# Three engines put in program order through the expert chunks, with weight splits traced one unit ahead and gather blocks spread out

## The chip, the core and the metric

The kernel runs on one core of a Trainium2 chip. The metric is the device time of one execution in microseconds (us), and a kernel's time is the median of several executions. A profile of one more execution gives the trace from which the rows below are taken. TensorE (PE) does the matrix products, its weight loads are listed apart as PEld, ScalarE is ACT, VectorE is DVE, GpSimd is POOL, and SyncE (SP) issues the large transfers from HBM.

## The reference, cut to what matters

Two layers are computed for 256 latent tokens (and 256 context tokens) of width 1024. Each layer has a mixer with four branches and then a channel mixer. The channel mixer of the first layer is dense; that of the second routes each token to two of eight experts:

```python
def swiglu(h, w1, w3, w2):
    return (jax.nn.silu(h @ w1) * (h @ w3)) @ w2

def moe_swiglu(h, router, w1, w3, w2):
    logits = (h @ router).astype(jnp.float32)
    top_v, top_i = lax.top_k(logits, TOP_K)          # TOP_K = 2
    probs = jax.nn.softmax(top_v, axis=-1)
    combine = ...                                    # (tokens, 8), zero where an expert wasn't chosen
    out = jnp.zeros_like(h)
    for e in range(N_EXPERTS):                       # 8
        out = out + combine[..., e:e + 1] * swiglu(h, w1[e], w3[e], w2[e])
    return out
```

An expert's w1 and w3 are 1024 x 3584 and its w2 is 3584 x 1024, all float32, so the eight experts hold 352 MB of weights, and each weight is read once. A final RMSNorm follows.

## The kernel before

The first part of the span does the mixers and the dense channel mixer. The change touches the second part only (`moe`), which begins with routing and then walks through the experts' weights.

**Experts and chunks.** The experts are put in slots by their load. Slots 1 to 3 are *heavy* (up to 128 tokens each), slots 0 and 4 to 7 are *light* (up to 64 tokens). Each expert's hidden width of 3584 is cut into seven chunks of 512. A chunk is six *units* of 1 MB: two of w1, two of w3, two of w2. The list `steps` puts the 56 chunks in one order: five light ones first, then heavy and light ones in turn, now and then two light ones in a row. No heavy chunk follows another directly, and two light chunks end the list.

**A light chunk** uses its raw float32 weights as they land (`light_first`: w1 and w3, 64 short matmuls in the trace's count, L1146; `light_turn`: two transposes, L1159, copied out by ScalarE, L1161; `light_second`: w2, 16 matmuls, L1173). Its gate is a Silu on ScalarE (L1150) and a product on VectorE (L1152).

**A heavy chunk** splits each weight unit in two float32r parts. `split` does it in halves of 128x1024: ScalarE copies (rounds) the half into `s1` (L145), then VectorE writes the remainder to `s2` (L146). Each product is then three matmuls (`mm3`, L176, L181, L182): high by high, high by low, low by high. L176 needs ScalarE's part of the split, L181 VectorE's. There are four buffers of `s1` and four of `s2`, so two units can be held split. `moe_first` multiplies w1 (two units), then w3 (two units), with Silu (L1096) and product (L1094). `moe_turn` transposes the result (L1105); ScalarE copies it to `G1` (L1108), VectorE takes the rest to `G2` (L1109). `moe_second` multiplies w2 (two units) into the banks `y`.

**How chunks interlock.** Work is late by a chunk on purpose: when heavy chunk c starts, the turn of heavy chunk c-1 comes first (`turns(True)`), then w1 of c, then in `heavy_aside(1)` the turn of the pending light chunk and w2 of c-1, then w3 of c. The w2 of a light chunk comes at the start of the next light chunk. At a light chunk's end, when a heavy one follows, the two w1 units of the heavy chunk are loaded and split in advance (`self.pre`). When an expert is done, `scatter` or `light_scatter` scales its `y` and adds it to the tokens (L1185 to L1210). The tokens of later experts are gathered (`gather`: eight blocks of four short matmuls, L1058, with XE and XL written by ScalarE and VectorE, then transposes); before, three such steps run after units 0, 2 and 3 of a heavy chunk.

**What sets the order.** Weights land in a ring of ten 1 MB buffers (`raw`, `mraw`); SP issues the next load when the buffer's last reader is done. A light unit's reader is TensorE; a heavy unit's is the split. TensorE's chunk matmuls and turns keep program order (`self.keep`), but everything on ScalarE and VectorE, and TensorE's gather and scatter matmuls, is laid in an order by a scheduler that simulates the kernel while it is built. `high_priority` moves loads and splits ahead in it. On the chip each engine then runs its own list from top to bottom.

Of the kernel before, what the change touches and what calls it, by code (L numbers as in the profile page):

```python
# [49 lines left out]
class Net:  # L50
# [1031 lines left out]
    def moe_first(self, src, XE, c, aside=lambda n: None):  # L1082

        nc = self.nc
        g = self.t2()
        for n, name in enumerate(("m_w1", "m_w3")):
            ps = self.bank(tag="mm")
            for kh in range(2):
                w = self.split_unit(src(name, c, kh))
                for kk in range(4):  # L1090
                    k = 4 * kh + kk
                    self.mm3(ps, (XE[:, 0, k], XE[:, 1, k]), w(512 * kk, 512 * kk + 512), k == 0, k == 7)
                if n == kh == 1:
                    nc.vector.tensor_tensor(g, g, ps, op=ALU.mult)  # L1094
                elif kh == 1:
                    nc.scalar.activation(g, ps, AF.Silu)  # L1096
                aside(2 * n + kh)
        return g

    def moe_turn(self, g):  # L1100

# [7 lines left out]
        nc.vector.tensor_tensor(G2, pt, G1.bitcast(F32), op=ALU.subtract)  # L1109
        return G1, G2  # L1110

    def moe_second(self, src, c, G, y, last=False, aside=lambda: None):
        G1, G2 = G
        for hb in range(2):
            self.cut = 2 if last and hb + self.ncut > 1 else 1
            w = self.split_unit(src("m_w2", c, hb))
            self.cut = 1
            for b in range(2):
                j = 2 * hb + b
                for hf in range(2):  # L1120
                    o = 1024 * b + 512 * hf
                    self.mm3(y[hf], (G1[:, j], G2[:, j]), w(o, o + 512), c == 0 and j == 0, c == EFF_CH - 1 and j == 3)
            if hb == 0:
                aside()

# [93 lines left out]
    def moe(self):  # L1219
        nc, E = self.nc, self.E  # L1220
        XE, PT, ready = {}, {}, set()

        def tables(i):
            tabs = (self.pos, self.sel, self.comb) if i == 0 else self.placed
            return [a[:, :2, i:i + 1] for a in tabs]

        def light(i, P):

            Q = E.tile([128, 2, 128], F32R, tag="Q", name=self.nm("Q"), bufs=1)
            nc.vector.memset(P[:, :, 192:].bitcast(F32), 0.0)  # L1230
            nc.vector.memset(Q[:, :, :64].bitcast(F32), 0.0)
            pos, sel, _ = tables(i)
            self.one_hot(P[:, :, 128:192], pos, sel)
            self.one_hot(Q[:, :, 64:], pos, sel)
            XE[i] = E.tile([128, 8, LCAP], F32, tag="XL", name=self.nm("XL"), bufs=2)
            PT[i] = E.tile([128, 2, 2, 128], F32R, tag="PTL", name=self.nm("PTL"), bufs=2)
            return Q

        def heavy(i, P):
            pos, sel, _ = tables(i)  # L1240
            self.one_hot(P[:, :, :128], pos, sel)
            XE[i], PT[i] = self.xe_tile(), self.pt_tile()

        def turn(i, P, Q=None):
            if Q is None:
                self.turned(PT[i], [P[:, t, :128] for t in range(2)])
            else:
                self.turned(PT[i].rearrange("p t h c -> p (t h) c"), [x for t in range(2) for x in (P[:, t, 128:], Q[:, t])])

        def gather(i, j):  # L1250

            P = E.tile([128, 2, 256], F32R, tag="P", name=self.nm("P"), bufs=1)
            if i:
                heavy(i, P)
            Q = light(j, P)
            yield from self.gather(P[:, :, 0 if i else 128:192], XE.get(i), XE[j])
            if i:
                turn(i, P)
            turn(j, P, Q)
            ready.update((i, j))  # L1260

        def begin():
            yield from gather(None, 0)
            self.weights()
            self.by_load()
            yield
            yield from gather(1, NH + 1)

        def run(gen, n=1000):
            for _ in range(n):  # L1270
                if next(gen, self) is self:
                    break

        big = lambda i: 0 < i <= NH
        side = begin()
        run(side, 9)
        hs, ls = ([(i, c) for i in p for c in range(EFF_CH)] for p in (range(1, NH + 1), [0, *range(NH + 1, NE)]))

        n = self.lead
        rest = [((k + 0.5) / len(q) * f, x) for q, f in ((hs, 0.95), (ls[n:], 1)) for k, x in enumerate(q)]  # L1280
        steps = ls[:n] + [x for _, x in sorted(rest, key=lambda a: a[0])]
        more = {(NH + k, 2): (k + 1 if k < NH else None, NH + k + 1) for k in range(1, NE - NH - 1)}

        def source(i):
            if i == 0:
                return lambda name, c, j: self.d[name][0, c, j]
            return lambda name, c, j, e=self.ids[i]: self.d[name][bass.ds(e, 1), c, j].rearrange("a p c -> (a p) c")
        y, g, G, late = {}, {}, {}, []
        todo = {True: [], False: []}

        def turns(kind):
            for x in todo[kind]:
                if x in g:
                    G[x] = (self.moe_turn if kind else self.light_turn)(g.pop(x))

        def puts():
            while late:
                run(late.pop(0))

        def second(kind, **kw):  # L1300

            while todo[kind] and todo[kind][0] in G:
                i, c = x = todo[kind].pop(0)
                if c == 0:
                    y[i] = self.ys() if kind else self.bank(tag="yl")
                (self.moe_second if kind else self.light_second)(source(i), c, G.pop(x), y[i], **kw)
                if c == EFF_CH - 1:
                    late.append((self.scatter if kind else self.light_scatter)(PT[i], y[i], tables(i)[2]))
                    run(late[-1], 1)

        def heavy_aside(n):
            if n == 1:
                turns(False)
                puts()
                second(True)
            else:
                run(side, 3)

        for m, (i, c) in enumerate(steps):
            kind = big(i)  # L1320
            if i == 0 and c == 4:
                self.gdma = False
                gf = self.O.tile([128, 2, 1024], F32, tag="gf", name="gf")
                self.g2, self.fg = self.gate(2, 0, gf[:, 0]), gf[:, 1]
                nc.scalar.dma_start(self.fg, self.d["fng"])
            if c == 0 and i not in ready:
                puts()
                run(side)
            after = steps[m + 1] if m + 1 < len(steps) else (0, 0)

            def light_aside(n):
                if n == 1:
                    turns(False)
                if n == 3 and big(after[0]):

                    if after[0] not in ready:
                        puts()
                        run(side)
                    src = source(after[0])
                    self.pre = [self.split_unit(src("m_w1", after[1], kh)) for kh in range(2)]  # L1340

            if kind:
                turns(True)
                g[i, c] = self.moe_first(source(i), XE[i], c, heavy_aside)
            else:
                second(False)
                g[i, c] = self.light_first(source(i), XE[i], c, light_aside)
                if not big(after[0]):
                    second(False)
            todo[kind].append((i, c))  # L1350
            if not kind and todo[True] and not any(big(x) for x, _ in steps[m:]):
                turns(True)
                second(True, aside=lambda: turns(False))
                puts()
            if (i, c) in more:
                puts()
                run(side)
                side = gather(*more[i, c])
        turns(False)
        second(False, last=True)  # L1360
        puts()

    def moe_rest(self):

# [351 lines left out]
```

## Time and profile before

| quantity | value |
|---|---|
| median of three runs | 1717.22 us (1715.92 to 1721.92) |
| the profiled execution's own time | 1717.08 us |
| its span in the trace | 1715.3 us |
| PE busy | 1623.0 us (95%) |
| VectorE busy | 960.1 us (56%) |
| ScalarE busy | 684.7 us (40%) |
| read from HBM | 478.86 MB |
| expert weight loads of 1 MB, issue to landing | 10.6 us (median) |

The span runs from the first to the last instruction; 1.8 us of the execution's own time lies around it. A matmul is counted as busy for longer than it keeps the next one waiting, so "PE busy" is high where PE merely runs. More telling are the stretches in which it waits, the granted clock (1.00 is 2.4 GHz, 0.50 is 1.2 GHz, and a stretch between them mixes the two), and the bytes that land per second. The expert part begins near 830 us and ends near 1702 us.

### The profile page before, as it was taken

What the parts mean: (1) busy time and instruction counts of PE and PEld (TensorE: products, weight loads), DVE (VectorE), ACT (ScalarE), POOL (GpSimd) and SP (SyncE); (2) the same over time, 40 slices, a digit from 0 to 9 for tenths busy, and PEclk for the clock granted to TensorE, in tenths of its full rate; (3) what the DMA queues carried; (4) which work ended last, traced back from release to release, by engine and by line L of the source; (5) the groups of instructions that cost most, each with busy time, mean ns of one, the idle gap of its engine ahead of it and who ended that gap; (6) DMA issues with size and microseconds to landing.
All of it is one profiled execution on the core that took longest, in us unless ns stands there. A gap on an engine that the chain in (4) does not pass through costs nothing. (4 is left out here: it accounts for less than half of the span.)

```text
span 1715.3 us, 23719 instructions
## 1 busy us (share of the span) xinstructions
PE 1623.0 (95%) x9333; PEld 1206.8 (70%) x9333; DVE 960.1 (56%) x1455; ACT 684.7 (40%) x1086; POOL 35.4 (2%) x46
## 2 busy tenths in 40 slices
PE   7999999999999999999899999998999899999986
PEld 4778799887787878899566566665766576665653
DVE  3769555567665697696233455455533464534343
ACT  4654344322222327655243344442533444433341
POOL 1000000000000030000000000000000000000000
PEclk8999999999999999999889999999999999999998
DMA  8543531534444433227899999999899999999992
GB/s 351 205 158 145 202 135 51 203 137 175 172 172 166 181 145 103 99 95 273 355 387 385 418 420 375 420 418 398 343 390 419 419 419 375 418 408 390 381 420 105
DMA packets 69030, 481.55 MB, mean 281 GB/s; under 512 B 8064, under 2 KB 8192, under 8 KB 12336
## 3 DMA queue, kind: packets, MB, share of 16 engines
q1 hardware_dynamic: 68480, 479.43, 70.6%
q8 instruction: 75, 1.23, 0.3%
q10 hardware_dynamic: 432, 0.54, 0.1%
q14 instruction: 43, 0.35, 0.1%
HBM read 478.86 MB, written 1.08 MB: 280 GB/s over the span
## 5 line engine op out<-in xcount | busy, mean ns | idle before, releaser
L146 DVE TENSOR_TENSOR s<-raw,s 128x1024 fp32r<-128x1024 f32 (+1 forms) x350 | 419.1, 1222 | 111.9 <-ACT s L145 110.0
L145 ACT CAST s<-raw 128x1024 fp32r<-128x1024 f32 (+1 forms) x350 | 357.9, 1050 | 275.3 <-PE mm L182 109.0
L176 PE MATMUL mm<-X,s 128*128 128x512 f32 (+1 forms) x672 | 247.1, 368 | 0.0
L181 PE MATMUL mm<-X,s 128*128 128x512 f32 (+1 forms) x672 | 247.0, 368 | 0.0
L182 PE MATMUL mm<-X,s 128*128 128x512 f32 (+1 forms) x672 | 245.8, 367 | 0.0
L1146 PE MATMUL mm<-raw,XL 128*64 128x256 f32 x1952 | 218.4, 380 | 0.0
L1146 PEld LDWEIGHTS mm<-raw,XL 128*64 128x64 f32 x1952 | 139.0, 137 | 81.2 <-issue 15.9
L176 PE MATMUL mm<-s,XE 128*128 128x512 f32 x336 | 141.2, 420 | 24.3 <-ACT s L145 24.3
L181 PE MATMUL mm<-s,XE 128*128 128x512 f32 x336 | 141.8, 422 | 9.5 <-DVE s L146 9.5
L176 PEld LDWEIGHTS mm<-X,s 128*128 128x128 f32 x672 | 126.4, 188 | 27.9 <-issue 6.7
L181 PEld LDWEIGHTS mm<-X,s 128*128 128x128 f32 x672 | 126.7, 189 | 26.0 <-issue 5.9
L182 PEld LDWEIGHTS mm<-X,s 128*128 128x128 f32 x672 | 126.5, 188 | 24.0 <-issue 3.4
L1150 ACT ACTIVATE t<-mm 128x256 f32<-128x256 f32 x35 | 13.4, 383 | 316.6 <-PE mm L1146 316.6
L182 PE MATMUL mm<-s,XE 128*128 128x512 f32 x336 | 139.0, 414 | 0.0
L1173 PE MATMUL yl<-raw,GL 128*64 128x512 f32 x488 | 111.2, 598 | 6.4 <-DVE t L1208 6.0
L1109 DVE TENSOR_TENSOR G<-sm,G 128x512 fp32r<-128x512 f32 x21 | 14.5, 691 | 168.7 <-ACT G L1108 168.7
L176 PEld LDWEIGHTS mm<-s,XE 128*128 128x128 f32 x336 | 67.1, 200 | 43.5 <-ACT s L145 27.8
L1152 DVE TENSOR_TENSOR t<-t,mm 128x256 f32<-128x256 f32 x35 | 14.6, 418 | 145.2 <-PE mm L1146 145.2
L181 PEld LDWEIGHTS mm<-s,XE 128*128 128x128 f32 x336 | 67.3, 200 | 30.5 <-DVE s L146 15.3
L176 PE MATMUL mm<-s,X 128*128 128x256 f32 (+1 forms) x304 | 86.5, 287 | 1.9 <-ACT mix L666 1.9
L181 PE MATMUL mm<-s,X 128*128 128x256 f32 (+1 forms) x304 | 86.0, 284 | 0.3 <-DVE s L146 0.3
L182 PE MATMUL mm<-s,X 128*128 128x256 f32 (+1 forms) x304 | 85.1, 285 | 0.0
(384 smaller groups left out, 2363.5 us busy)
## 6 DMA issues: line engine op xcount, KB each, us to landing
raw<-in_m_w_dram SPq DMA_DIRECT2D x294, 1024.0 KB, 10.6
mraw<-in_mod_w_dram SPq DMA_DIRECT2D x47, 1024.0 KB, 4.8
raw<-in_f_w_dram SPq DMA_DIRECT2D x33, 1024.0 KB, 4.9
mraw<-in_m_w_dram SPq DMA_DIRECT2D x32, 1024.0 KB, 11.7
raw<-in_w_in_dram SPq DMA_DIRECT2D x20, 1024.0 KB, 4.8
raw<-in_w_out_dram SPq DMA_DIRECT2D x8, 1024.0 KB, 4.9
first<-in_m_w_dram SPq DMA_DIRECT2D x8, 512.0 KB, 8.9
once<-in_m_w_dram SPq DMA_DIRECT2D x3, 1024.0 KB, 16.1
```

Source lines behind the costliest of these rows:

```text
L145: self.last = (nc.scalar.copy(s1[:, :h], r), nc.vector.tensor_tensor(s2[:, :h], r, s1[:, :h].bitcast(F32), op=ALU.subtract))
L146: nc.vector.tensor_tensor(s2[:, :h], r, s1[:, :h].bitcast(F32), op=ALU.subtract))
L176: m = mm(out, a[0], b[0], start=first, stop=False)
L181: self.keep(mm(out, a[0], b[1], start=False, stop=False))
L182: self.keep(mm(out, a[1], b[0], start=False, stop=last))
L1109: nc.vector.tensor_tensor(G2, pt, G1.bitcast(F32), op=ALU.subtract)
L1146: self.keep(nc.tensor.matmul(ps[64 * b:64 * b + 64], XL[:, k], w(o, o + 256), start=(k == 0), stop=(k == 7), tile_position=(0, 64 * b)))
L1150: nc.scalar.activation(g, ps, AF.Silu)
L1152: self.keep(nc.vector.tensor_tensor(g, g, ps, op=ALU.mult))
L1173: self.keep(self.nc.tensor.matmul(y[64 * hf:64 * hf + 64], G[:, b, 64 * hb:64 * hb + 64], w(o, o + 512), start=(c == 0 and hb == b == 0), ...
```

## The change

On TensorE, ScalarE and VectorE every instruction traced between the start of the chunk loop and its end gets a dependency on the one traced before it on the same engine, so that the scheduler can only lay them down in the order in which the Python code calls them. (SP and POOL are left to the scheduler.) Since the order of the code now is the order on the engine, the code is rearranged. A list `plan` holds the units that the next heavy chunk needs: w1, w1, w2 and w2 of the chunk before, w3, w3. `look_ahead` takes one and traces its load and its split. Two are traced at the end of the light chunk ahead of the heavy one, and one more after each unit's matmuls. The same is done for the w2 of the last heavy chunk. Gather steps run one after each unit of a heavy chunk, and one in the middle of w2. When an expert's last w2 is done, `second` returns instead of going on to the next expert, and scatters are put after w1 or after w3 of a heavy chunk, or at the very end.

```diff
@@ moe_first
-                w = self.split_unit(src(name, c, kh))
+                w = self.split_ahead(src(name, c, kh))
...
                 elif kh == 1:
                     nc.scalar.activation(g, ps, AF.Silu)
+                self.look_ahead()
                 aside(2 * n + kh)
         return g
+
+    def split_ahead(self, src):
+        return self.pre.pop(0) if self.pre else self.split_unit(src)
+
+    def look_ahead(self):
+
+        if self.plan:
+            src, cut = self.plan.pop(0)
+            pre, self.pre, self.cut = self.pre, [], cut
+            pre.append(self.split_unit(src))
+            self.pre, self.cut = pre, 1
@@ moe_second
-            w = self.split_unit(src("m_w2", c, hb))
+            w = self.split_ahead(src("m_w2", c, hb))
...
+            self.look_ahead()
             if hb == 0:
                 aside()
@@ moe
                     late.append((self.scatter if kind else self.light_scatter)(PT[i], y[i], tables(i)[2]))
                     run(late[-1], 1)
+                    return
 
         def heavy_aside(n):
             if n == 1:
                 turns(False)
                 puts()
-                second(True)
-            else:
-                run(side, 3)
-
+                second(True, aside=lambda: run(side, 1))
+            elif n == 3:
+                puts()
+            run(side, 1)
+
+        self.plan = []
+        traced = nc.cur_bb.bb.instructions
+        begun = len(traced)
...
                     src = source(after[0])
-                    self.pre = [self.split_unit(src("m_w1", after[1], kh)) for kh in range(2)]
+                    self.plan = [(src(x, after[1], kh), 1) for x in ("m_w1", "m_w3") for kh in range(2)]
+                    if todo[True]:
+                        i, c = todo[True][0]
+                        self.plan[2:2] = [(source(i)("m_w2", c, hb), 1) for hb in range(2)]
+                elif n == 3 and todo[True] and not any(big(x) for x, _ in steps[m:]):
+                    i, c = todo[True][0]
+                    self.plan = [(source(i)("m_w2", c, hb), 1) for hb in range(2)]
+                if n == 3:
+                    for _ in range(2):
+                        self.look_ahead()
...
                 second(True, aside=lambda: turns(False))
-                puts()
...
+        puts()
         turns(False)
         second(False, last=True)
         puts()
+
+        last = {}
+        for x in list(traced[begun:]):
+            if x.engine in (mybir.EngineType.PE, mybir.EngineType.Activation, mybir.EngineType.DVE):
+                if x.engine in last:
+                    self.tc.add_manual_dep(x, last[x.engine].name, mybir.DependencyInfo(
+                        mybir.DependencyClass.NoSync, mybir.DependencyReason.DATA), reason="issue_after")
+                last[x.engine] = x
```

The first place is ScalarE's list at the start of a heavy chunk (the fifth of the second heavy expert). `raw_10540` and `raw_10550` are its two w1 units, `G` the copy of the turned chunk before it, and `t_1916<-mm_10571` its Silu. Before:

```order
L1150 ACTIVATE t_1896_10496<-mm_10497 128x256
L1108 CAST G_1914_10566<-sm_10561 128x512
L145 CAST s_1904_10542<-raw_10540 128x1024
L145 CAST s_1906_10546<-raw_10540 128x1024
L145 CAST s_1909_10552<-raw_10550 128x1024
L145 CAST s_1911_10556<-raw_10550 128x1024
L145 CAST s_1921_10604<-raw_10602 128x1024
L145 CAST s_1923_10608<-raw_10602 128x1024
L145 CAST s_1926_10626<-raw_10624 128x1024
L145 CAST s_1928_10630<-raw_10624 128x1024
L1096 ACTIVATE t_1916_10570<-mm_10571 128x512
```

The same place now, where `raw_10584` and `raw_10607` are the w2 units that were `raw_10602` and `raw_10624`:

```order
L1161 ACTIVATE t_1896_10496<-mm_10497 128x256
L145 CAST s_1904_10542<-raw_10540 128x1024
L145 CAST s_1906_10546<-raw_10540 128x1024
L145 CAST s_1909_10552<-raw_10550 128x1024
L145 CAST s_1911_10556<-raw_10550 128x1024
L1120 CAST G_1914_10566<-sm_10561 128x512
L145 CAST s_1919_10586<-raw_10584 128x1024
L145 CAST s_1921_10590<-raw_10584 128x1024
L1096 ACTIVATE t_1916_10570<-mm_10571 128x512
L145 CAST s_1924_10609<-raw_10607 128x1024
L145 CAST s_1926_10613<-raw_10607 128x1024
```

The copy G (L1108, now L1120) stood ahead of the four w1 copies and now stands behind them; the Silu (L1096) stood behind both w2 units and now stands between them.

The second place is ScalarE's list ahead of the last heavy chunk's w2 (`raw_13015` and `mraw_13042` before). Before:

```order
L1150 ACTIVATE t_2446_12961<-mm_12962 128x256
L1108 CAST G_2454_13011<-sm_13006 128x512
L145 CAST s_2457_13017<-raw_13015 128x1024
L145 CAST s_2459_13021<-raw_13015 128x1024
L145 CAST s_2464_13044<-mraw_13042 128x1024
L145 CAST s_2466_13048<-mraw_13042 128x1024
```

And now, where these units are `raw_13005` and `mraw_13015`:

```order
L1161 ACTIVATE t_2446_12961<-mm_12962 128x256
L145 CAST s_2454_13007<-raw_13005 128x1024
L145 CAST s_2456_13011<-raw_13005 128x1024
L145 CAST s_2459_13017<-mraw_13015 128x1024
L145 CAST s_2461_13021<-mraw_13015 128x1024
L1120 CAST G_2464_13031<-sm_13026 128x512
```

Here too G goes from the front of the four copies to their end.

## Rows read from the trace of the kernel before

**Rows 1.** The page, part 2: GB/s in 40 slices of 42.9 us.
```profile
GB/s 351 205 158 145 202 135 51 203 137 175 172 172 166 181 145 103 99 95 273 355 387 385 418 420 375 420 418 398 343 390 419 419 419 375 418 408 390 381 420 105
```

**Rows 2.** The chain that ended last: start us, us, engine, tile, line.
```profile
1653.08 0.23 PE mm L181
...
1661.27 6.91 PE mm L1146 x64
...
1695.02 3.68 PE yl L1173 x16
1698.72 0.68 DVE t L1208
```

**Rows 3.** Stretches: us, busy per engine (instructions), clock, DMA share, GB/s.
```profile
840.00:1681.00 841.00, 787.66 (x4495) 526.76 (x4490) 387.29 (x445) 326.56 (x436) 0.00 (x0) 0.97 0.98 399
915.00:1681.00 766.00, 715.19 (x4039) 483.33 (x4036) 363.97 (x404) 302.76 (x394) 0.00 (x0) 0.97 0.98 402
895.00:900.00 5.00, 5.00 (x24) 4.00 (x23) 4.18 (x4) 3.80 (x6) 0.00 (x0) 1.00 0.46 146
1200.00:1205.00 5.00, 5.00 (x23) 4.03 (x22) 4.46 (x4) 3.63 (x4) 0.00 (x0) 1.00 0.25 64
1680.00:1685.00 5.00, 4.42 (x18) 1.94 (x19) 3.88 (x6) 0.44 (x1) 0.00 (x0) 1.00 0.15 59
```

**Rows 4.** Waits of SP's queue, 915 to 1681: us in total, times, longest.
```profile
SPq L119 <- DVE s L146: 249.3, 89, 8.6
SPq L119 <- PE yl L1173: 142.9, 56, 7.2
```

**Rows 5.** Waits of PE and ACT, 790 to 1715: us in total, times, longest.
```profile
PE mm L176 <- ACT s L145: 24.3, 15, 1.6
PE mm L181 <- DVE s L146: 9.5, 16, 0.8
PE yl L1173 <- DVE t L1208: 6.0, 4, 1.5
PE y L176 <- ACT s L145: 1.6, 1, 1.6
ACT s L145 <- DMA raw<-in_m_w_dram: 3.9, 3, 2.7
```

**Rows 6.** Timeline, a heavy chunk's start with a wait: start us, us, [idle before].
```profile
1292.83 0.66 PE L1105 MATMUL sm<-ident,t 128*128 128x128 f32 x4
1293.52 0.59 ACT L1108 CAST G<-sm 128x512 fp32r<-128x512 f32 x1 [3.65 <-PE sm L1105]
1294.00 3.89 ACT L145 CAST s<-raw 128x1024 fp32r<-128x1024 f32 x4
1295.11 0.49 PE L176 MATMUL mm<-s,XE 128*128 128x512 f32 x1 [1.62 <-ACT s L145]
1296.36 0.50 PE L181 MATMUL mm<-s,XE 128*128 128x512 f32 x1 [0.77 <-DVE s L146]
```

**Rows 7.** Timeline, a heavy chunk's start without a wait.
```profile
1257.76 2.00 ACT L145 CAST s<-raw 128x1024 fp32r<-128x1024 f32 x2
1261.41 0.48 PE L176 MATMUL mm<-s,XE 128*128 128x512 f32 x1
1261.69 0.59 ACT L1108 CAST G<-sm 128x512 fp32r<-128x512 f32 x1 [1.93 <-PE sm L1105]
1267.41 0.60 ACT L1096 ACTIVATE t<-mm 128x512 f32<-128x512 f32 x1 [1.35 <-PE mm L182]
1268.16 4.90 ACT L145 CAST s<-raw 128x1024 fp32r<-128x1024 f32 x5
```

**Rows 8.** Stretches at two heavy starts, PE alone: busy, clock, DMA share, GB/s.
```profile
1294.10:1302.10 8.00, 6.23 (x19) 0.79 1.01 420
1334.10:1342.10 8.00, 6.24 (x27) 1.00 1.00 416
```

**Rows 9.** The page, part 5: VectorE's half of a split, mean ns.
```profile
L146 DVE TENSOR_TENSOR s<-raw,s 128x1024 fp32r<-128x1024 f32 (+1 forms) x350 | 419.1, 1222 | 111.9 <-ACT s L145 110.0
```

More of the change, by code (lines that the diff above doesn't have):

```diff
@@ L1110, in moe_turn, with moe_second @@
         return G1, G2
-    def moe_second(self, src, c, G, y, last=False, aside=lambda: None):
+    def moe_second(self, src, c, G, y, aside=lambda: None):
         G1, G2 = G
         for hb in range(2):
-            self.cut = 2 if last and hb + self.ncut > 1 else 1
-            w = self.split_unit(src("m_w2", c, hb))
-            self.cut = 1
+            w = self.split_ahead(src("m_w2", c, hb))
             for b in range(2):
```

## Prediction, made before the changed kernel was run

> **What bounds the kernel now.** I read the page's bandwidth slices first. The second half of the span moves weights at up to 420 GB/s, with dips to 343 and 364 and a last slice of 105 [rows 1]. So the expert part runs close to the rate of its own loads, yet not at it. The stretches say how far off: from 915 us, when the first heavy chunks are under way, to 1681 us, when the last weights land, 402 GB/s, against 420 in an undisturbed piece [rows 3, 8]. The loss is in a few holes (64 GB/s at 1200 to 1205, 146 at 895 to 900), and TensorE shows 5.00 us of 5 busy in both [rows 3]: loads pause while TensorE works.
>
> What a load waits for is next. SP's queue waits 249.3 us for VectorE's splits and 142.9 us for the light chunks' w2 matmuls [rows 4], the last readers of ring buffers. In the other direction hardly anybody waits for weights: ScalarE's copies waited for landing data three times in all, 3.9 us [rows 5]. So the ring is full of landed units, and TensorE's progress sets the pace.
>
> TensorE's waits are then what matters. Two have one shape: L176 waits for ScalarE's part of a split 15 times, 24.3 us, at most 1.6 each, and L181 for VectorE's part 16 times, 9.5 us [rows 5]. The timeline shows the place, the start of a heavy chunk [rows 6]. ScalarE sits idle 3.65 us for the transposes of the chunk before, because the copy G (L1108) heads its list; the splits of the w1 units, whose data is there, stand behind it. TensorE does the transposes, then waits 1.62 us for the first half's copy and 0.77 us for its remainder. There is a counter-example in the same trace: at another start ScalarE's list had two w1 copies ahead of G (1257.76 against 1261.69), and L176 starts at 1261.41 with no wait [rows 7]. The order alone makes the difference.
>
> Such a wait has an aftermath. In the 8 us around the start of rows 6 the granted clock is 0.79 and 19 matmuls are recorded; around a start where it stayed at 1.00, 27 [rows 8]. Cutting the same stretch around all 15 starts gives 0.79 nine times and 1.00 six times. A mean of 0.79 over 8 us is 3.4 us at 1.2 GHz, so 1.7 us of work lost.
>
> **The change part by part.** The sum is made against the profiled execution, 1717.08 us with a span of 1715.3; the median of 1717.22 is the same within 0.2 us.
>
> *TensorE's side.* (a) G moves behind the four w1 copies on ScalarE, as in rows 7 but for both units. The 15 waits go: 24.3 + 9.5 = 33.8 us. What is late next is G itself: four copies take 3.89 us [rows 6] and can run while the light chunk's last 64 matmuls (6.91 us [rows 2]) still go on, so G comes straight after the transposes, and its reader, w2, starts 24 matmuls (5.6 us at 0.23 [rows 2]) later. (b) At nine starts 1.7 us of half-clock work goes: 15 us; bounds 0 (the clock falls anyway) and 766 x 0.03 / 0.5 / 2 = 23 us (all of the 0.97 of rows 3 at half clock while working). I take 15, from the count. (c) The last heavy chunk's w2 has the same wait once, 1.6 us [rows 5], and about 0.8 behind it as at the others [rows 6]: 2.4. (d) A new light expert's w2 waited four times, 6.0 us, for the scatter to empty its bank [rows 5]. Since `second` now returns when an expert is done, a heavy chunk lies between: 6.0. Together 33.8 + 15 + 2.4 + 6.0 = 57 us; the w2 matmuls that end at 1698.7 [rows 2] could end at 1642 if weights always were there.
>
> *Gathers.* The same 32 matmuls per gather are spread over two heavy chunks instead of one; nothing is added. The new cost could be a wait for bank or copy at each of five blocks a chunk; the chunk's other matmuls stand between blocks, so I put zero, at most 1.2 us for each of three gathers.
>
> *The loads' side.* SP's order of loads stays nearly what it was, and a load still waits for its buffer. At 420 GB/s the bytes from 915 to 1681 need 766 x 402 / 420 = 733 us, so the last weights can land at 1648, not before, if the hole at 895 to 900 (still with TensorE's start-up behind it) stays. That is later than 1642, so the loads are the bound from some point on. TensorE needs 766 - 57 = 709 us for what the loads need 733: it gains 3% on them, and to use up a backlog of some six landed units (15 us at 2.5 us each, 1.05 MB at 420 GB/s) takes 15 / 0.03 = 500 us. For the first 500 us the ring is nearly full, and a gather or a scatter can still make a hole. Of the 33 us of holes I leave 6: last landing 1654; bounds 0 and 15.
>
> The Trainium skill (DMA: Bandwidth & Descriptors, Specifications) gives an HBM limit of about 358 GB/s per core and a fabric ceiling of 435. By the first the same bytes would need 860 us, and nothing could be gained; by the second 708. The trace's 420 contradicts the first, so the floor stays at 733.
>
> *After the last landing.* Now 17.7 us pass from 1681 to 1698.7, since TensorE is behind by a light chunk's matmuls. With TensorE waiting for weights, what follows the last landing is at most the last w2's 3.68 us [rows 2]; the chunk's first part has the two units before it (5 us) to finish. I take 4 (bounds 2, and 8 at half clock). From there to the end of the span it is 1715.3 - 1698.7 = 16.6 us as now; the scatter's order within it changes by less than 1 us.
>
> Sum: 1654 + 4 + 16.6 = 1674.6 span, + 1.8 around it = 1676.4; I say **1677 us**, 40 us faster.
>
> **Rivals.**
>
> *The clock eats part of it.* Once TensorE outruns the loads it must wait for them, and in rows 8 such pauses bring 1.2 GHz. If all 21 heavy starts lose 1.7 us instead of nine, that is 21 us more on TensorE: 1642 + 21 = 1663, later than the loads' 1648. With 4 for the catch-up, 3 for an end at half clock: 1670 + 16.6 + 1.8 = 1688. For it: nine of 15 starts do so now. Against: a wait for a bound load costs nothing by itself, and work that lands meanwhile is done afterwards at full clock. The Trainium skill (TensorE: Matmul & The Clock Gate, HAM oscillation — how this bites in real kernels) describes such a kernel, throttled again at every tile by its wait for DMA; by it this rival is the rule, by the six starts at 1.00 it is not.
>
> *The full floor.* No hole after 915, and the hole at 895 halved (3 us): 1645 + 2 + 16.6 + 1.8 = 1665. Against: three gathers and eight scatters still come in lumps.
>
> *The Silu takes G's place (slower).* In the new list L1096 stands between the two w2 units. It waits for the last w1 matmul, and the second w2 unit's copy waits behind it. Chain: 0.59 for the Silu [rows 7], 3.89 / 4 = 0.97 for a copy [rows 6], 1.22 for its remainder [rows 9], 2.8 us; cover: the first w2 unit's 12 matmuls x 0.23 = 2.8 us and two transposes of the light chunk. The margin is thin. If it fails by today's 2.4 us with the clock's 1.7 behind it in all 21 chunks, 86 us come and 57 go: 1717 + 29 = 1746. It decides from 57 / 21 = 2.7 us per chunk. Against: in rows 7 the list before had the Silu (1267.41) ahead of copies of that w2 unit too, and L176's wait for w2 splits came once in the whole part, at the very end [rows 5].
>
> *It does nothing.* If the w1 units hadn't landed when ScalarE now turns to them, their wait would only change its name: 1717. Against: copies wait for data 3.9 us in all [rows 5].
>
> **How the numbers follow.** Forecast 0.60, own range 1666 to 1690; clock 0.18; full floor 0.10; Silu 0.07, of it 0.05 slower and 0.02 about even; nothing 0.05. Faster is 0.60 + 0.18 + 0.10 = 0.88, same 0.02 + 0.05 = 0.07, slower 0.05; by over 0.3% (5 us) each, about what a measurement can tell here. The range 1660 to 1703 takes in the floor, the clock's rival and half of (a) failing (17 us and the clock behind it).
>
> **What would show it.** Right: the waits of L176 and L181 at heavy starts fall from 33.8 us to a few or turn into waits for DMA; ScalarE's and SP's lists show waits for landing weights well above 3.9 us in the second half; bandwidth from 915 on is at least 412 GB/s; last weights land near 1654; under 6 us lie between that and the last w2 matmul. Wrong: L176 or L181 on `y` waits 21 times behind L1096 (Silu); clock below 0.95 over the part with loads under 410 GB/s (clock); holes as deep as before with the ring full, which would mean that TensorE's waits were not what held the loads.

## The result and the profile after

The changed kernel takes 1691.39 us (median of four runs, 1690.79 to 1692.21), the kernel before, run on the same chip, 1719.1. The ratio is 0.984, 95% interval 0.9819 to 0.9861: faster by 28 us, where 40 were forecast. The profiled execution after has a span of 1689.1 us.

Bandwidth by slices, from the page of the kernel after (part 2, 40 slices of 42.2 us):

```profile
GB/s 363 195 164 150 180 162 51 184 140 189 160 174 138 207 154 101 125 76 205 335 417 315 419 418 413 405 418 419 418 395 398 419 420 412 418 419 419 419 420 168
```

The dips of before (343, 375 and others below 400 [rows 1]) have shrunk to 395 and 398, save one of 315 near 900 us; most slices stand at 417 to 420. The same in stretches, after, with columns as in [rows 3]:

```profile
840.00:915.00 75.00, 70.44 (x426) 41.34 (x424) 18.44 (x37) 19.31 (x38) 0.00 (x0) 0.91 0.89 351
915.00:1660.00 745.00, 709.63 (x4092) 482.50 (x4090) 366.23 (x416) 302.32 (x398) 0.00 (x0) 0.98 1.01 415
1660.00:1665.00 5.00, 5.00 (x50) 3.34 (x48) 0.00 (x0) 0.38 (x1) 0.00 (x0) 1.00 0.29 117
```

From 915 us on 415 GB/s land, before 402 [rows 3]. In the last of these stretches 117 GB/s x 5 us = 0.59 MB come, 1.4 us at 420: the last weights land near 1661.4. From there 11 us pass to the end of the last w2 matmul, 1672.55, and 16.55 more to the end of the span.

TensorE's waits in the expert part, after (us in total, times, longest), which answer to [rows 5]:

```profile
PE mm L1208 <- DVE res L1211: 12.2, 4, 3.1
PE sm L1058 <- DVE P L1047: 10.4, 4, 3.4
PE sm L1073 <- ACT XL L1066: 5.1, 3, 2.3
PE y L176 <- ACT G L1120: 5.0, 1, 5.0
...
PE mm L176 <- ACT s L145: 2.1, 2, 1.6
PE mm L181 <- DVE s L146: 2.0, 3, 0.8
```

The two waits at heavy starts fell from 24.3 and 9.5 us to 2.1 and 2.0. The first four rows, 32.7 us in all, were not there at this size. The other end of the ring, ScalarE and SP after (the second for 915 to 1660):

```profile
ACT s L145 <- DMA raw<-in_m_w_dram: 12.5, 8, 4.7
```
```profile
SPq L119 <- DVE s L146: 171.6, 64, 9.5
...
SPq L119 <- DMA raw<-in_m_w_dram: 92.4, 61, 2.6
```

ScalarE now waits for weights that haven't landed (12.5 us, before 3.9 [rows 5]), and SP waits for transfers in the queue for 92.4 us, where it waited for none in the same stretch before. Its waits for splits fell from 249.3 [rows 4] to 171.6 us. So for a part of the time it is now the transfers that hold up the next load, and no longer their readers.

The start of [rows 6], the same chunk after (timeline: start us, us, instruction, [idle before]):

```profile
1285.92 3.88 ACT L145 CAST s<-raw 128x1024 fp32r<-128x1024 f32 x4
...
1288.97 0.66 PE L1117 MATMUL sm<-ident,t 128*128 128x128 f32 x4
1289.39 0.48 PE L176 MATMUL mm<-s,XE 128*128 128x512 f32 x1
1289.69 0.58 ACT L1120 CAST G<-sm 128x512 fp32r<-128x512 f32 x1
```

The copies start 3 us ahead of the transposes; L176 follows these with no wait, and G comes behind the copies, 0.06 us after the transposes end (1289.63).

### The profile page after: what moved, and what is told of

Read it like the earlier page. It is cut to its first block, busy times and chain, and to the rows that moved or that the text cites. A ratio compares the mean times of both kernels' runs of the same rounds, so it can differ in the third digit from the quotient of the medians.

```text
span 1689.1 us, 23700 instructions
## 1 busy us (share of the span) xinstructions
PE 1608.9 (95%) x9333; PEld 1202.3 (71%) x9333; DVE 955.9 (57%) x1455; ACT 679.7 (40%) x1086; POOL 35.4 (2%) x46
## 5 line engine op out<-in xcount | busy, mean ns | idle before, releaser
L146 DVE TENSOR_TENSOR s<-raw,s 128x1024 fp32r<-128x1024 f32 (+1 forms) x350 | 414.9, 1221 | 272.2 <-ACT s L145 271.6
L145 ACT CAST s<-raw 128x1024 fp32r<-128x1024 f32 (+1 forms) x350 | 355.4, 1050 | 277.6 <-PE mm L181 98.0
L176 PE MATMUL mm<-X,s 128*128 128x512 f32 (+1 forms) x672 | 247.2, 368 | 0.0
L181 PE MATMUL mm<-X,s 128*128 128x512 f32 (+1 forms) x672 | 247.0, 368 | 0.0
L176 PEld LDWEIGHTS mm<-X,s 128*128 128x128 f32 x672 | 126.4, 188 | 27.9 <-issue 6.7
L181 PEld LDWEIGHTS mm<-X,s 128*128 128x128 f32 x672 | 126.7, 189 | 26.0 <-issue 5.9
L176 PE MATMUL mm<-s,XE 128*128 128x512 f32 x336 | 139.2, 414 | 2.2 <-ACT s L145 2.1
L181 PE MATMUL mm<-s,XE 128*128 128x512 f32 x336 | 136.4, 406 | 2.0 <-DVE s L146 2.0
L182 PE MATMUL mm<-s,XE 128*128 128x512 f32 x336 | 135.9, 404 | 0.0
L176 PE MATMUL mm<-s,X 128*128 128x256 f32 (+1 forms) x304 | 86.5, 287 | 2.0 <-ACT mix L666 2.0
L181 PE MATMUL mm<-s,X 128*128 128x256 f32 (+1 forms) x304 | 86.0, 285 | 0.8 <-DVE s L146 0.8
L1184 PEld LDWEIGHTS yl<-raw,GL 128*64 128x64 f32 x488 | 33.0, 137 | 63.6 <-issue 62.0
L176 PEld LDWEIGHTS mm<-s,XE 128*128 128x128 f32 x336 | 65.6, 195 | 17.3 <-ACT s L145 3.1
L181 PEld LDWEIGHTS mm<-s,XE 128*128 128x128 f32 x336 | 65.5, 195 | 17.4 <-DVE s L146 3.1
## 6 DMA issues: line engine op xcount, KB each, us to landing
once<-in_m_w_dram SPq DMA_DIRECT2D x3, 1024.0 KB, 16.1
```

The lines of the kernel that those rows point to most:

```text
L145: self.last = (nc.scalar.copy(s1[:, :h], r), nc.vector.tensor_tensor(s2[:, :h], r, s1[:, :h].bitcast(F32), op=ALU.subtract))
L146: nc.vector.tensor_tensor(s2[:, :h], r, s1[:, :h].bitcast(F32), op=ALU.subtract))
L176: m = mm(out, a[0], b[0], start=first, stop=False)
L181: self.keep(mm(out, a[0], b[1], start=False, stop=False))
L182: self.keep(mm(out, a[1], b[0], start=False, stop=last))
L1184: self.keep(self.nc.tensor.matmul(y[64 * hf:64 * hf + 64], G[:, b, 64 * hb:64 * hb + 64], w(o, o + 512), start=(c == 0 and hb == b == 0), ...
```

## The experiments

Each ratio is to the kernel before on the same chip, with its 95% interval. Medians of runs on different chips differ by up to 3 us for the same kernel (before: 1716 to 1719), so what tells two versions apart is the ratios; a difference of medians is called one.

**The place of G.** In e1 the kernel before is left as it is, but for a hold: `behind` makes the scheduler lay G behind the last weight copy traced before it.

```diff
@@ moe_turn (kernel before)
-        nc.scalar.copy(G1, pt)
+        with self.behind(self.last[:1]):
+            nc.scalar.copy(G1, pt)
```

> The kernel before with one thing altered: ScalarE's copy G of a turned heavy chunk is held behind the last weight copy traced ahead of it, so that it stands behind the four w1 copies. No pins, no new trace order, gathers as before. Theory (the place of G is the cause): the waits of L176 and L181 at heavy starts fall from 33.8 us to under 8, bandwidth from 915 on rises from 402 to at least 413 GB/s, and the time falls by 20 to 32 us (1687 to 1699). Rival (the gain comes from program order as such, or from gathers and scatters being placed otherwise): less than 8 us.

Measured: 1681.02 us, ratio 0.9794 (0.976 to 0.9827), span 1678.4. One hold gives 35 us by the medians, at least as much as the whole change, and more than the 20 to 32 expected. Its waits and its main stretch:

```profile
PE yl L1174 <- DVE t L1209: 6.0, 4, 1.5
PE mm L181 <- DVE s L146: 5.3, 8, 1.4
PE mm L1198 <- ACT Y L1210: 4.9, 2, 2.7
...
PE mm L176 <- ACT s L145: 4.5, 7, 1.1
```
```profile
915.00:1650.00 735.00, 704.63 (x4060) 472.44 (x4056) 363.60 (x408) 302.66 (x393) 0.00 (x0) 0.99 1.01 417
```

L176 and L181 lose 24 us of their 33.8 (9.8 are left, under 8 were expected), and the granted clock goes from 0.97 to 0.99. The other waits stand as they did: the scatter's for Y is 4.9 us in both traces, so there is no sign that the rest of the schedule moved. The wait of the light w2 (6.0 us, part (d) of the forecast) is still there and does no visible harm. Loads land at 417 GB/s.

In e2 the change stays and only G goes back to the front: the turn is called before the two units of the next chunk are looked ahead, so that G and its remainder on VectorE stand ahead of their splits.

```diff
@@ light_aside (kernel after)
                     src = source(after[0])
+                    turns(True)
                     self.plan = [...]
```

> The changed kernel with one thing undone: the turn of the heavy chunk before is traced ahead of the two w1 splits, so G again heads ScalarE's list at a heavy start; everything else of the change stays. Theory (place of G): 20 waits of 1.62 and 0.77 us come back, 40 to 48 us on TensorE, on top of the changed kernel's own new waits (12.2 us on L1208, 10.4 on L1058, 5 on L1073); time 1715 to 1740, no faster than before. Rival (G's place doesn't matter): 1688 to 1696.

Measured: 1765.59 us, ratio 1.0281 (1.0259 to 1.0304). With program order everywhere, the wait of [rows 6] stands at all 21 starts. One of them, and the sums:

```profile
1327.33 0.58 ACT L1120 CAST G<-sm 128x512 fp32r<-128x512 f32 x1 [3.65 <-PE sm L1117]
1327.81 3.89 ACT L145 CAST s<-raw 128x1024 fp32r<-128x1024 f32 x4
...
1328.91 0.50 PE L176 MATMUL mm<-s,XE 128*128 128x512 f32 x1 [1.62 <-ACT s L145]
```
```profile
PE mm L176 <- ACT s L145: 34.0, 21, 1.6
PE mm L181 <- DVE s L146: 15.7, 21, 0.8
```
```profile
915.00:1650.00 735.00, 662.22 (x3665) 447.84 (x3661) 335.33 (x383) 276.26 (x363) 0.00 (x0) 0.95 0.93 378
```

Against the kernel after 74 us come by the medians (70 between the two profiled executions) in 21 places, 3.3 to 3.5 us each. The traces account for 68 of them: 49.7 us of waits where the kernel after has 4.1, and by the granted clock (0.98 to 0.95 over 735 us, rounded rows) 22 us of lost work. The forecast had 48.8 / 15 = 3.3 us per start for the two. The expectation had reckoned with the waits alone, and the time came out 25 us above its range. So G's place is the cause, in both directions, and its price was about right.

**The pins.** In e3 the loop at the end that adds the dependencies is gone; the code's new order stays.

```diff
-        last = {}
-        for x in list(traced[begun:]):
...
-                last[x.engine] = x
```

> The changed kernel without the dependencies that keep program order: new trace order, look-ahead, gathers and returns stay, the scheduler orders the engines. In its list G stands ahead of most w1 copies again. Theory (place of G): the waits of L176 behind L145 come back to 20 us or more, time 1705 to 1722. Rival (the new trace order brings the gain, the pins nothing): 1688 to 1696.

Measured: 1705.2 us, ratio 0.995 (0.9928 to 0.9973). The scheduler puts G ahead of the copies again; ScalarE sits idle for the transposes before all 21 copies G, 76.1 us in all, and in the kernel after before none:

```profile
PE mm L176 <- ACT s L145: 26.7, 18, 1.6
PE mm L181 <- DVE s L146: 12.4, 18, 0.8
```

Order in the code alone brings about a third of the gain; what the pins add is that ScalarE keeps to it. The waits at the gathers and scatters (L1058 for P, L1208 for L1211) are 0.7 and 0.4 us in this trace: they belong to the pins.

**What the floor is.** In e4 the third product of each heavy triple is left out, 504 matmuls x 0.233 us = 117 us of TensorE's work.

```diff
@@ mm3 (kernel after)
         self.keep(m)
+        if self.kept:
+            self.keep(mm(out, a[0], b[1], start=False, stop=last))
+            return
```

> The changed kernel with the third product (low by high) of each heavy triple left out, which takes 21 x 24 x 0.2325 = 117 us of work from TensorE; loads, splits and order stay. Theory (the loads are the bound in the changed kernel): bandwidth from 915 on 418 to 421 GB/s, last landing 1645 to 1656, the time falls by only 8 to 25 us against the changed kernel (1666 to 1683), TensorE waits for landing weights instead. Rival (TensorE is still the bound): the time falls by over 60 us.

Measured: 1679.98 us, ratio 0.9776 (0.9754 to 0.9798): 117 us less work for TensorE gives 11 us. The stretch:

```profile
915.00:1650.00 735.00, 646.21 (x3602) 386.30 (x3600) 365.87 (x416) 302.22 (x398) 0.00 (x0) 0.96 1.01 418
```

418 GB/s at 646 us of TensorE's busy time: the loads are the bound after the change, and 418 to 420 is what they give here.

**The end.** In e5 G of the last heavy chunk goes back ahead of its w2 copies, everything else as after.

```diff
                 elif n == 3 and todo[True] and not any(big(x) for x, _ in steps[m:]):
+                    turns(True)
                     i, c = todo[True][0]
```

> The changed kernel with the last heavy chunk's turn traced ahead of its two w2 splits, so that there alone G comes first again. Theory (G behind splits whose data has not landed costs 5.0 + 0.7 us and a spell at half clock near the end): that wait shrinks to at most 2.4 us, last landing stays near 1661, the time falls by 2 to 7 us against the changed kernel (1684 to 1689). Rival (the end hangs on the last landing, the wait is absorbed): within 1.5 us of it.

Measured: 1687.09 us, ratio 0.9828 (0.9809 to 0.9847). By the intervals that is not told apart from the kernel after (4.3 us by the medians, 2 by the ratios); the trace shows it, the kernel after first:

```profile
1641.00 1.99 ACT L145 CAST s<-raw 128x1024 fp32r<-128x1024 f32 x2 [4.69 <-DMA raw<-in_m_w_dram]
...
1643.49 1.99 ACT L145 CAST s<-mraw 128x1024 fp32r<-128x1024 f32 x2 [0.50 <-DMA mraw<-in_m_w_dram]
...
1645.39 0.58 ACT L1120 CAST G<-sm 128x512 fp32r<-128x512 f32 x1
1646.02 0.79 PE L176 MATMUL y<-s,G 128*128 128x512 f32 x1 [5.01 <-ACT G L1120]
```

And e5:

```profile
1642.23 0.58 ACT L1120 CAST G<-sm 128x512 fp32r<-128x512 f32 x1 [4.70 <-PE sm L1117]
1642.72 1.99 ACT L145 CAST s<-raw 128x1024 fp32r<-128x1024 f32 x2
...
1643.82 0.49 PE L176 MATMUL y<-s,G 128*128 128x512 f32 x1 [1.62 <-ACT s L145]
```

After, G waits behind four copies of weights that are only landing, though its own input was ready at 1641.0; with G first the wait is 1.62 in place of 5.01. The last w2 starts at 1665.54 us in e5, in place of 1668.90.

**The lumps.** In e6 the light scatter is traced one unit earlier, ahead of the look-ahead's splits, a gather's one-hot tiles are traced when it is set up, and its transposes get a step of their own.

```diff
+                if n < kh:
+                    soon()          # puts
                 self.look_ahead()
@@ heavy_aside
                 turns(False)
-                puts()
@@ gather
+            if j > NH + 1:
+                yield
             yield from self.gather(...)
+            if j > NH + 1:
+                yield
@@ steps
                 side = gather(*more[i, c])
+                run(side, 1)
```

> The changed kernel with three new waits taken away: a light expert's scatter is traced ahead of the split that VectorE had in front of its additions (L1208 behind L1211, 12.2 us), a gather's one-hot matrices are traced when it is created and not in front of its first block (L1058 behind L1047, 10.4 us), and a step lies between a gather's last block and its transposes (L1073 behind L1066, 5.1 us). Theory (these lumps make the 9 us of holes after 915): these waits fall under 6 us together, bandwidth from 915 on rises from 415 to 417 to 419 GB/s, last landing 1653 to 1658, the time falls by 3 to 8 us (1683 to 1688). Rival (the ring hides them): within 1.5 us.

Measured: 1683.98 us, ratio 0.9814 (0.9794 to 0.9833), against the kernel after 7.4 us by the medians, 4.5 by the ratios, again inside the intervals. Its waits and the stretch of one gather, 1030 to 1060, where the kernel after had clock 0.94 and 407 GB/s:

```profile
PE mm L176 <- ACT s L145: 7.2, 7, 1.6
...
PE sm L1058 <- DVE P L1047: 5.6, 4, 2.1
PE y L176 <- ACT G L1122: 5.0, 1, 5.0
...
PE mm L1210 <- DVE res L1213: 1.1, 2, 0.6
```
```profile
1030.00:1060.00 30.00, 30.00 (x205) 20.19 (x206) 12.53 (x18) 11.80 (x20) 0.00 (x0) 1.00 1.01 419
```

The 12.2 us of L1208 fell to 1.1, the 10.4 of L1058 to 5.6, and with them the holes went: 419 GB/s from 915 to 1650. The waits of L176 and L181 at heavy starts rose meanwhile from 4.1 to 14.0 us, and the time fell all the same.

**The first heavy start.** In e7 the splits of the first heavy chunk's w1 are traced ahead of the gather that is forced there.

```diff
                 if n == 3 and big(after[0]):
-                    if after[0] not in ready:
-                        puts()
-                        run(side)
...
                         self.look_ahead()
+                if n == 3 and big(after[0]) and after[0] not in ready:
+                    puts()
+                    run(side)
```

> The changed kernel with the first heavy chunk's w1 splits traced ahead of the gather that runs in one go there. Theory (in program order these splits stand behind the gather's copies, which cost 1.62 + 0.47 us and half clock at 893 and moved 1.4 MB fewer bytes by 915): wait gone, 2 to 4 us faster than the changed kernel. Rival (ring full there, nothing to gain): within 1.5 us.

Measured: 1694.7 us, ratio 0.9873 (0.9853 to 0.9892), and 333 GB/s from 840 to 915 where after has 351. The idea was wrong: the time is no shorter than that of the kernel after (the intervals overlap). The wait of L176 there is gone, and this one came, in e7:

```profile
886.41 2.03 PE L1058 MATMUL sm<-P,H 128*128 128x192 f32 x8 [3.69 <-DVE P L1047]
```

VectorE has the splits' remainders ahead of the one-hots now, and the gather stands behind those. The three edits together (e8):

> The changed kernel with the edits of the three runs beside it together. Theory (loads are the floor, what is left above it are these lumps and the tail): the gains add up to 8 to 15 us, last landing 1649 to 1655, time 1676 to 1683, about that of the kernel before with G alone held back (ratio to before 0.976 to 0.983). Rival (each lump is hidden by the next): 1687 to 1692.

Measured: 1682.73 us, ratio 0.98 (0.9781 to 0.982); 418 GB/s from 915, 329 before it. The start-up's loss is paid here too.

**The look-ahead.** In e9 only the w1 units are looked ahead; w2 and w3 are split where they are used.

```diff
-                    self.plan = [(src(x, after[1], kh), 1) for x in ("m_w1", "m_w3") for kh in range(2)]
-                    if todo[True]:
-                        i, c = todo[True][0]
-                        self.plan[2:2] = [(source(i)("m_w2", c, hb), 1) for hb in range(2)]
+                    self.plan = [(src("m_w1", after[1], kh), 1) for kh in range(2)]
```

> The changed kernel, still in program order, with only the two w1 units traced ahead; w2 and w3 are split where they are used. ScalarE's list then has the Silu and the light chunk's copy in front of the first w2 unit's copies. Theory (a list run from top to bottom makes any copy behind a waiting instruction late): L176 on y waits about 1.6 us and L181 0.8 us in each of about 20 heavy chunks, 40 to 50 us in all, and the time is 1740 to 1770, as in the run with G first. Rival (one unit ahead is not needed, the w1 splits were all): within 5 us of the changed kernel.

Measured: 1821.49 us, ratio 1.0612 (1.0588 to 1.0637), far above what was expected. Its waits:

```profile
PE y L176 <- ACT s L145: 38.5, 22, 2.2
PE mm L176 <- ACT s L145: 31.6, 15, 3.7
PE y L181 <- DVE s L146: 25.3, 26, 2.1
PE mm L181 <- DVE s L146: 9.8, 15, 0.8
```

I had counted w2 (the rows with `y`) alone, and w3 is late as well (most of the rows with `mm`): 105 us of waits, and the granted clock from 915 to 1650 is 0.92. In program order a split that is not traced ahead is a wait each time; the look-ahead is not an extra but what pays for the pins.

**The gather's steps.** In e10 three blocks run at a time after units 0, 2 and 3, as in the kernel before, instead of one per unit.

```diff
-                second(True, aside=lambda: run(side, 1))
+                second(True)
             elif n == 3:
                 puts()
-            run(side, 1)
+            if n != 1:
+                run(side, 3)
```

> The changed kernel with the gather steps back to three after units 0, 2 and 3 of a heavy chunk. Theory (spreading them out costs and gains next to nothing): within 3 us of the changed kernel (1688 to 1694), L1058's wait for L1066 up by 2 to 6 us. Rival (the spread is a part of the gain): over 5 us slower.

Measured: 1704.96 us, ratio 0.9932 (0.9912 to 0.9952). The theory (no difference) fell, the rival was right: in the pinned kernel over half of the gain hangs on the spreading. One gather, 1050 to 1060, in e10 and then after:

```profile
1050.00:1060.00 10.00, 8.28 (x36) 4.59 (x36) 2.33 (x7) 3.11 (x8) 0.00 (x0) 0.83 0.24 100
```
```profile
1050.00:1060.00 10.00, 10.00 (x90) 6.04 (x86) 0.42 (x1) 0.38 (x1) 0.00 (x0) 1.00 0.98 383
```

36 matmuls in place of 90, and 100 GB/s in place of 383. SP waits for splits there, 16.1 us from 1030 to 1064, once 12.7 at a time. Over 915 to 1650 it is 406 GB/s in place of 415.

**What can be had.** e11 takes e5 and e6 and a start in another order (one-hots, splits, then blocks).

> The changed kernel with the tail and the lumps mended as before, and the start in another way: there the gather's one-hot matrices come first on VectorE, then the w1 splits, then the gather's blocks. Theory (in the run that failed, the splits only took the matrices' place in the queue, 3.69 us): that wait and the 1.62 us are both gone, bytes by 915 no fewer than before the change, time 1674 to 1680. Rival (start-up is set by the full ring): as tail and lumps together, 1679 to 1683.

Measured: 1680.32 us, ratio 0.9791 (0.9771 to 0.9812), below the interval of the kernel after. From 840 to 915 it has 339 GB/s, still fewer than before's 367, so the start was not gained.

e12 has the order of the code after, no pins, the hold of e1 on G and the line of e5.

> The changed kernel's trace order without the pins, G held behind the last traced copy instead, and the tail mended. Theory (G's place is all; the scheduler deals with the lumps): waits of L176 and L181 at starts under 10 us, bandwidth from 915 on 416 to 420 GB/s, time 1674 to 1682, as good as the best pinned version. Rival (pins matter beyond G): 1686 to 1692.

Measured: 1679.5 us, ratio 0.9783 (0.9764 to 0.9802), also below the interval of the kernel after; it is the lowest median, and e1, e11 and e12 can't be told apart. Its stretches:

```profile
840.00:915.00 75.00, 72.47 (x460) 43.48 (x458) 23.30 (x41) 23.78 (x43) 0.00 (x0) 0.93 0.93 368
915.00:1650.00 735.00, 708.45 (x4100) 472.23 (x4096) 358.03 (x404) 300.84 (x395) 0.00 (x0) 1.00 1.01 418
```

The start is as before (368), the rest at the loads' rate. Under 10 us were expected for the waits of L176 and L181 at heavy starts; there are 17.4, and the time is no worse for it. So the pins are not needed for the gain, and neither is the code's new order (e1).

## Why the prediction was right, and where its sizes were off

The direction and the cause held: G's place, shown both ways by e1 and e2. So did the bound: the loads, by e4. What was too small is two terms of the sum 1654 + 4 + 16.6, which came out as 1661.4 + 11.1 + 16.55 = 1689.1. The time of 1691.39 us lies 1.4 above the forecast's own range (1666 to 1690), inside the wide one (1660 to 1703). Of the signs named for "right" three came, the waits at the starts, the waits for weights and the bandwidth; the last landing near 1654 and the short end after it did not. One reading was wrong without consequence: [rows 1] has no dip to 364; beside 343 it has two of 375.

**(a) The waits at heavy starts: right.** 33.8 us became 4.1, G stands where it was said to, and no w2 waits for it except at the end.

**(b) The clock: right in sign, and not separable.** The granted clock from 915 on went from 0.97 [rows 3] to 0.98; over the same 745 us that is 7 us of work by the rounded rows, half of the 15 taken. As the loads bind, it no longer sets the time: e4 has 0.96 and is faster. What e2 adds per start, 3.3 to 3.5 us against 3.3 reckoned, agrees with the price of wait and aftermath together.

**(c) The last heavy chunk: wrong.** "2.4 us gone" became 5.0 + 0.7 us. The order showed G behind four copies, and I read the place as I read the others, where the weights had landed. At the end they had not: once TensorE keeps up with the loads, the last copies wait for data, and G waits with them. This follows from the forecast's own statement that weights would be late, and I didn't carry it to this place.

**(d) The light w2: right, and worth little.** The 6.0 us went; e1 keeps them and is as fast as any version.

**The last landing, 7.4 us late.** The term was 733 us of pure transfer plus 6 of holes from 915. The 733 rested on 915 being reached with the same bytes. It was not: from 840 to 915 there came 351 GB/s in place of 367 before (the same stretch of that trace), 1.2 MB, 2.9 us. The first heavy start shows why TensorE is late there, after:

```profile
891.87 1.99 ACT L145 CAST s<-raw 128x1024 fp32r<-128x1024 f32 x2
...
892.97 0.79 PE L176 MATMUL mm<-s,XE 128*128 128x512 f32 x1 [1.62 <-ACT s L145]
```

The forced gather is in front, and the splits stand behind its copies, where the scheduler had fitted them in between. e7, e8 and e11 moved this and did not gain it; the pinned runs of this section have 329 to 359 GB/s there. The pins alone need not be it, as e3 without them has 357 and e12 368; how to order the start under pins is open. Next, 415 against 420 over 745 us are 8.9 us of holes, not 6. The remaining 1.6 us lie within the rounding of these rows: half a GB/s over 745 us is 0.4 MB, 0.9 us, in either trace. The forecast's landing could be had: in e1, with 373 GB/s at the start and 417 after, 265 GB/s x 5 us = 1.3 MB come from 1650 on, and the last weights land near 1653.

**Gathers "zero, at most 1.2 us for each", and no term for scatters: the step that failed.** With program order on VectorE too, the tile that TensorE needs stands behind work traced earlier. A light scatter after:

```profile
992.64 2.36 DVE L146 TENSOR_TENSOR s<-raw,s 128x1024 fp32r<-128x1024 f32 x2 [1.89 <-ACT s L145]
...
994.91 2.72 DVE L1211 SCALAR_TENSOR_TENSOR res<-mm,comb,res 128x512 f32<-128x512 f32 x4
995.71 0.50 PE L1208 MATMUL mm<-Y,PTL 128*128 128x512 f32 x1 [3.06 <-DVE res L1211]
```

And a gather:

```profile
1026.54 2.35 DVE L146 TENSOR_TENSOR s<-raw,s 128x1024 fp32r<-128x1024 f32 x2
...
1029.92 0.71 PE L1058 MATMUL sm<-P,H 128*128 128x192 f32 x4 [3.42 <-DVE P L1047]
```

In both a split that was traced ahead (2.36 us of VectorE) stands in front of the small instruction that TensorE waits for: 2.9 to 3.4 us, seven times (four scatters, three gathers). It is the pattern of [rows 6] on another engine, made by the look-ahead. I had looked for a wait on bank or copy and not read VectorE's list at these places. e6 takes most of these waits away and is 4.5 to 7.4 us faster, inside the intervals. Nor was the spreading of the gathers neutral: under the pins it is worth 14 us (e10), and the forecast had nothing for it.

**After the last landing, 11.1 us instead of 4.** I had counted the last w2 alone. From 1661.4, TensorE is still 4.5 us in the light chunk's first part; then comes a scatter, 1665.91 to 1668.06, two transposes and the wait for GL, 0.84 us; then w2 with 3.65:

```profile
1668.90 3.65 PE L1184 MATMUL yl<-raw,GL 128*64 128x512 f32 x16 [0.46 <-ACT GL L1172]
```

Of the 7 us too few, 3.0 are the scatter and turn between w3 and w2, which need no weights and could have been counted from the code. Of the 4.5, e5 shows 3.4 to be (c)'s; why TensorE is about 1 us late beyond that is not shown.

**The rivals.** The clock's rival gave 1688, near what was measured, but by a sum that was short: the 1642 it starts from has the 15 us of (b) taken off already, so that 21 starts of 1.7 us add 36 us to it and not 21, and the rival's time is 1703. Nor did its way come: it asked for 1.7 us at all 21 starts, a clock below 0.95 and under 410 GB/s, and the trace has 0.98 and 415. The Trainium skill (TensorE: Matmul & The Clock Gate, HAM oscillation — how this bites in real kernels) describes a throttle brought back by every wait for DMA; here TensorE itself waited for a landing weight once, 0.6 us, so the page's case did not arise. In e12 it waited so twelve times, 4.7 us in all and at most 0.5 at a time, and the granted clock from 915 to 1650 was 1.00. The Silu's rival did not come: w2 units wait for no split in the kernel after. Nor did the third: the waits went, they didn't change their name. The full floor (1665) was not reached by any version; the best stand at 1680.

On bandwidth, the forecast weighed 358 GB/s per core and put it aside. The Trainium skill (HBM Reference, Specifications (TRN2)) adds that a core streaming alone measures about 425; the 418 to 420 of these traces, on one core, agree with that sentence.

## What to carry to other kernels

An engine that runs its list in order turns every early wait into a wait of all that stands behind it. Before pinning an order, read at each place that another engine waits for what stands ahead of it on the list and whether its input is there at that time, on every pinned engine and at the first and last round too. Try one hold at the place that the trace names before ordering a whole program: here one hold gave at least what the whole rearrangement gave. And price a rearrangement by what it adds to every list: here the look-ahead (e9) and the spreading (e10) were needed to make up for the pins.

## What the runs showed that I had not expected

How little TensorE's work matters once loads bind: 117 us less of it gave 11 us (e4). And how much a few microseconds of order matter before that: moving one copy of 0.58 us per heavy chunk by four places on ScalarE's list is worth 35 us one way (e1, on the kernel before) and 74 the other (e2, on the kernel after).
